# Latent attention: logits from high and low parts, rotated query columns first, values per four heads

## The chip, the cores and the metric

The kernel runs on one core of a Trainium2 chip. The metric is device time in microseconds. The kernel before took 2329.86 us (median of three runs, 2329.52 to 2330.2). Engines are named as the profile names them: PE is TensorE's matrix product, PEld its weight load, DVE is VectorE, ACT is ScalarE, POOL is GpSimd and SP is SyncE, which here only issues DMAs.

## The reference

The reference is a long chain: a first block (sparse attention, a pooling mixer, a mixture of 16384 experts), then two layers with residuals. The second of these layers has the latent attention (`mla`), the only part that the change touches. The sequence has 512 tokens, the model width is 1024, everything is fp32.

```python
proj = u @ w_in                                  # 384 | 256 | 32 | 1024 columns
cq, ckv, k_rope, z = split(proj)
q  = (rms_norm(cq, q_norm) @ w_qb).reshape(B, S, 16, 64 + 32)   # nope | rope
kv = (rms_norm(ckv, kv_norm) @ w_kvb).reshape(B, S, 16, 64 + 64) # k_nope | v
q_rope, k_rope = rotate(q_rope), rotate(k_rope)  # k_rope is shared by the 16 heads
logits = (qn @ k_nope.T + qr @ k_rope.T) * 96 ** -0.5
o = softmax(logits) @ v                          # for each of 16 heads
y = (o * silu(z)) @ w_out
```

So each of 16 heads has a 512x512 logit matrix over 96 columns, no mask, a softmax over keys, and a product with 64 value columns.

## The kernel before, in words

A matrix product of full fp32 operands takes two pieces on PE. The kernel avoids that for its large products: an operand is split into a high part, rounded to the type float32r (FR in the code), and a low part, the difference. ACT writes the high part by a copy, DVE or POOL subtracts to get the low part, and `mm3` (line 152) adds three one-pass products, high by high, high by low and low by high. `panel` (line 142) loads a block of weights, up to 256 rows by 512 columns, and splits it; three raw panels (WB) and four split ones (WS) can be held at once. `linear_tm` and `linear_fm` (lines 180 and 188) run such a projection with tokens or features on the partitions, and call an `evac` function for each finished part.

The logits of the latent attention are the exception: keys and queries are plain fp32 tiles of 96 rows (64 nope rows, 32 rotated), and line 1154 makes one logit block of 128 queries by 512 keys with one fp32 product, which the profile shows as two pieces.

The stage runs as follows. After the z projection (`evac_z`), the normed latents cq and ckv are transposed (`latents`, called between the value parts). The value projection makes all 16 heads' values in two calls of 512 columns, into the tiles vB: 64 high columns and 64 low columns for each head and token block. `four_heads` (line 1133) makes keys and queries of four heads: first the key projection (`evac_k`), then the query projection (`evac_q`), whose three parts of 128 columns are two of nope columns and one, the last, with the rotated columns of the four heads. That last part goes through a rotation: three DVE operations, an addition on POOL (line 1124), and eight DMAs on SP's queue (line 1127) that move the rows into the four query tiles. KB = 6 key tiles and as many query tiles form two rings.

`b_head` (line 1146) runs one head in four units of 128 queries. A unit is: the logit product into a PSUM tile, a maximum on DVE (1156), an exponential on ACT that also sums (1158), four transposes on PE (1161), a high part on ACT (1163) and a low part on DVE (1164). After two units, PE multiplies by the values (1170). Each head ends with a copy, an addition and a reciprocal; every second head also transposes four blocks of zB (1192) and multiplies by them.

The loop over heads calls `four_heads(j + 1)` ahead of the third head of each four (`m == 2`), so that it can be worked on beside the heads. The order on each engine is not written by hand: a planner walks the program with its own estimate of times and gives each engine its next instruction by readiness and by the order in the source. On the chip each engine then follows its own list strictly. PSUM tiles are tagged: `acc` has four buffers, for projections, transposed exponentials and outputs alike; `lg` and `tp` have two each, for logits by turns.

After the heads come the output projection (w_out) with its weights loaded early, a per-layer-embedding step `ple`, and the final norm; they reuse tiles of the stage by tag.

## Time and profile before

| | |
|---|---|
| median of three runs | 2329.86 us |
| the profiled execution, its own time | 2336.29 us |
| its span (first to last instruction) | 2334.1 us |
| granted TensorE clock, mean share of full | 0.984 |
| busy: PE, DVE, ACT, POOL | 2241.3, 1623.3, 1114.2, 1051.2 us |
| latent attention, start of the values to the last value product | 2034 to 2219.8 us |

The durations of single instructions come from the one profiled execution. PE's products are pipelined: a product's own length is longer than the time from one to the next, so costs on PE are read from the distance between starts or from the chain of waits, which counts each piece only as long as it holds the chain. "Granted clock" is the share of 2.4 GHz that TensorE got in a stretch.

### The profile page before, as it was taken

How to read it: one execution, taken by the hardware profiler on the slowest of the kernel's cores; microseconds unless marked ns; L12 is line 12 of the kernel's file. 1: busy time of each engine (PE TensorE's matmuls, PEld its weight loads, DVE VectorE, ACT ScalarE, POOL GpSimd, SP SyncE). 2: the span in 40 equal slices, each digit the busy share in tenths (PEclk: the TensorE clock that was granted, in tenths of full speed). 3: DMA queues.
4: the chain of work that ended last, by engine and by line, in shares of the span. 5: the costliest groups of instructions: out<-in, count | busy, mean ns of one | idle time of the engine just before them, and what ended most of it. 6: DMA issues, size and time to landing. Idle time of an engine off the chain costs nothing.

```text
span 2334.1 us, 32581 instructions
## 1 busy us (share of the span) xinstructions
PE 2241.3 (96%) x11610; PEld 1930.8 (83%) x11610; DVE 1623.3 (70%) x2962; ACT 1114.2 (48%) x2134; POOL 1051.2 (45%) x642
## 2 busy tenths in 40 slices
PE   7999999998999899999999999999999999989998
PEld 5777778988999899999997788887889789767676
DVE  7695447889585654888887988888565445347755
ACT  3656323436757675333332333333456444467742
POOL 4874034574545565778876655564110100121100
PEclk9999999999999999999999999999999999999999
DMA  7465122376767788999998999996410233211121
GB/s 277 145 204 184 60 77 79 124 236 207 257 244 259 247 297 308 341 342 342 334 336 303 340 327 342 327 336 234 129 39 18 82 108 97 74 49 53 33 82 63
DMA packets 206482, 463.04 MB, mean 198 GB/s; under 512 B 17680, under 2 KB 99056, under 8 KB 203248
## 3 DMA queue, kind: packets, MB, share of 16 engines
q1 hardware_dynamic: 169456, 326.72, 41.9%
q0 software_dynamic: 36864, 134.23, 15.8%
q8 instruction: 92, 1.51, 0.3%
q14 instruction: 70, 0.57, 0.1%
HBM read 415.26 MB, written 44.58 MB: 197 GB/s over the span
## 4 chain that ended last, share of the span: by engine, by line
PE 70%; DVE 9%; DMA 6%; issue 6%; POOL 4%; ACT 3%; SPq 0%; POOLq 0%; DVEq 0%; ACTq 0%
PE acc L155 16%; PE acc L154 16%; PE acc L153 15%; PE gp L680 3%; PE tp L155 2%; PE tp L154 2%; PE tp L153 2%; PE lg L154 2%; PE lg L153 2%; PE lg L155 2%; DMA g<-in_peer_v_dram,idx 2%; PE lg L1154 2%; DVE oh L666 1%; POOL wada L271 1%; POOL wlo L716 1%
## 5 line engine op out<-in xcount | busy, mean ns | idle before, releaser
L716 POOL TENSOR_TENSOR wlo<-wraw,whi 128x1024 fp32r<-128x1024 f32 x172 | 441.7, 2570 | 397.0 <-ACT whi L715 388.2
L715 ACT ACTIVATE whi<-wraw 128x1024 fp32r<-128x1024 f32 x256 | 268.9, 1051 | 153.5 <-PE lg L154 73.2
L153 PE MATMUL acc<-fm,whi 128*128 128x384 f32 (+2 forms) x932 | 333.3, 359 | 1.6 <-ACT av L728 1.3
L155 PE MATMUL acc<-fm,wlo 128*128 128x384 f32 (+2 forms) x932 | 322.5, 348 | 3.0 <-POOL wlo L716 2.9
L154 PE MATMUL acc<-fm,whi 128*128 128x384 f32 (+2 forms) x932 | 323.1, 347 | 0.0
L751 DVE CUSTOM_DVE_ANT_0 g<-g,h20y 128x1024 f32<-128x1024 f32 x128 | 197.5, 1548 | 120.5 <-DMA g<-in_peer_u_dram,idx 120.3
L790 ACT ACTIVATE wh<-w 128x384 fp32r<-128x384 f32 x128 | 67.2, 525 | 360.2 <-DVE w L787 345.1
L148 ACT ACTIVATE whi<-wraw 128x1024 fp32r<-128x1024 f32 (+5 forms) x142 | 138.4, 981 | 160.4 <-PE acc L155 89.2
L149 POOL TENSOR_TENSOR wlo<-wraw,whi 128x1024 fp32r<-128x1024 f32 (+4 forms) x48 | 104.4, 2183 | 240.1 <-ACT whi L148 231.5
L154 PE MATMUL acc<-wlo,wh 128*128 128x512 f32 x512 | 203.7, 398 | 5.1 <-POOL wlo L716 5.1
L761 DVE SCALAR_TENSOR_TENSOR h20y<-g,act,h20y 128x1024 f32<-128x1024 f32 x127 | 192.5, 1516 | 17.7 <-DMA g<-in_peer_v_dram,idx 17.2
L155 PE MATMUL acc<-whi,wl 128*128 128x512 f32 x512 | 204.0, 398 | 0.0
L153 PEld LDWEIGHTS acc<-fm,whi 128*128 128x128 f32 x932 | 178.3, 192 | 11.6 <-issue 2.2
L149 DVE TENSOR_TENSOR wlo<-wraw,whi 128x1024 fp32r<-128x1024 f32 (+3 forms) x94 | 109.2, 1169 | 113.1 <-ACT whi L148 109.5
L155 PEld LDWEIGHTS acc<-fm,wlo 128*128 128x128 f32 x932 | 177.7, 191 | 11.4 <-POOL wlo L716 4.2
L154 PEld LDWEIGHTS acc<-fm,whi 128*128 128x128 f32 x932 | 178.4, 192 | 9.0 <-issue 2.2
L734 POOL DMA_INDIRECT g<-in_peer_u_dram,idx x128 | 172.9, 1351 | 26.5 <-issue 14.5
L734 POOL DMA_INDIRECT g<-in_peer_v_dram,idx x128 | 160.7, 1255 | 34.6 <-issue 21.5
L153 PE MATMUL acc<-whi,wh 128*128 128x512 f32 x512 | 171.7, 396 | 0.5 <-ACT whi L715 0.4
L669 ACT ACTIVATE oh<-oh,gT 128x128 f32<-128x128 f32 x384 | 120.1, 392 | 77.4 <-DVE oh L666 77.2
L153 PE MATMUL acc<-whi,fm 128*128 128x512 f32 (+3 forms) x368 | 135.9, 375 | 3.3 <-ACT fm L139 2.1
L791 DVE TENSOR_TENSOR wl<-w,wh 128x384 fp32r<-128x384 f32 x128 | 113.2, 884 | 35.9 <-ACT wh L790 33.9
(367 smaller groups left out, 5512.8 us busy)
## 6 DMA issues: line engine op xcount, KB each, us to landing
wraw<-in_uT_dram SPq DMA_DIRECT2D x128, 512.0 KB
wraw<-in_peer_v_dram SPq DMA_DIRECT2D x128, 512.0 KB
wada<-in_w_adaT_dram SPq DMA_DIRECT2D x48, 512.0 KB
G_d<-stage SPq DMA_DIRECT2D x24, 1024.0 KB
gm<-G_d SPq DMA_DIRECT2D x64, 384.0 KB
A_d<-av SPq DMA_DIRECT2D x88, 192.0 KB
am<-A_d SPq DMA_DIRECT2D x88, 192.0 KB
wraw<-in_w_in_dram SPq DMA_DIRECT2D x24, 512.0 KB
```

The source lines that it names most:

```text
L148: nc.scalar.activation(hi[:, :nk, :n], raw[:, :nk, :n], AF.Copy)
L149: eng.tensor_sub(lo[:, :nk, :n], raw[:, :nk, :n], hi[:, :nk, :n].bitcast(FT))
L153: nc.tensor.matmul(o, lh, rh, start=first, stop=False)
L154: nc.tensor.matmul(o, lh, rl, start=False, stop=False)
L155: nc.tensor.matmul(o, ll, rh, start=False, stop=last)
L669: nc.scalar.activation(oh[:, 1, i], oh[:, 1, i], AF.Copy, scale=gT[:, q * 4 + i:q * 4 + i + 1])
L715: nc.scalar.activation(hi, raw, AF.Copy)
L716: eng.tensor_sub(lo, raw, hi.bitcast(FT))
L734: tc.keep_in_program_order(nc.gpsimd.indirect_dma_start(out=g, out_offset=None, in_=src, in_offset=bass.IndirectOffsetOnAxis(ap=idx0[:, s: ...
L751: nc.vector.tensor_tensor_reduce(out=g, in0=g, in1=h20, scale=1.0, scalar=0.0, op0=OP.mult, op1=OP.add, accum_out=act0[:, i:i + 1])
L761: nc.vector.scalar_tensor_tensor(y, g, act0[:, s:s + 1], y, op0=OP.mult, op1=OP.add)
L791: nc.vector.tensor_sub(wl, w, wh.bitcast(FT))
```

## The change

Keys and queries become tiles of two parts, `[P, 2, S]` in float32r, high and low; `evac_k` and `evac_q` write the low part with a DVE subtraction after ACT's copy. The fixed rotated key rows are split once for each key tile. The logit product becomes `mm3` over 96 rows. In the weights' layout the rotated query columns come first in a group, and `four_heads` makes queries ahead of keys. The rotation's addition moves from POOL to DVE; its eight DMAs now go to a tile rs, from which ACT and DVE write the high and low rows. KB goes from 6 to 5. The values are made per four heads (256 columns at a time), the first four heads' before the loop and the others' beside `four_heads(j + 1)`, which is now called ahead of the last head of each four (`m == 3`). Some tiles of the tail take other tags.

```diff
-KB = 6
+KB = 5
...
+    def evac_v(vB, t, p):
         v = p.rearrange("p (h d) -> p h d", d=64)
-        nc.scalar.activation(vB[j][t][:, :, 0:64], v, AF.Copy)
-        nc.vector.tensor_sub(vB[j][t][:, :, 64:128], v, vB[j][t][:, :, 0:64].bitcast(FT))
+        to = vB[t // 2][:, t % 2]
+        nc.scalar.activation(to[:, :, 0:64], v, AF.Copy)
+        nc.vector.tensor_sub(to[:, :, 64:128], v, to[:, :, 0:64].bitcast(FT))
+
+    def values(j, then=None):
+        vB = [tmp.tile([P, 2, 4, P], FR, name="vB", tag=("h", "gain")[j % 2], bufs=2) for _ in range(2)]
+        linear_tm(A["b_w_v"][0], 2, j * 256, 256, cT, NT, lambda t, p: evac_v(vB, t, p), k_at=3,
+                  by_part=True, then=then)
+        return vB
...
     def evac_k(kB, m, p):
         for a in range(2):
-            nc.scalar.activation(kB[2 * m + a][0:64], p[a * 64:(a + 1) * 64], AF.Copy)
+            hi, lo = kB[2 * m + a][:, 0], kB[2 * m + a][:, 1]
+            own = p[a * 64:(a + 1) * 64]
+            nc.scalar.activation(hi[0:64], own, AF.Copy)
+            nc.vector.tensor_sub(lo[0:64], own, hi[0:64].bitcast(FT))
 
     def evac_q(qB, m, p):
-        if m < 2:
+        if m:
             for a in range(2):
-                nc.scalar.activation(qB[2 * m + a][0:64], p[a * 64:(a + 1) * 64], AF.Copy, scale=B_SCALE)
+                hi, lo = qB[2 * (m - 1) + a][:, 0], qB[2 * (m - 1) + a][:, 1]
+                own = p[a * 64:(a + 1) * 64]
+                nc.scalar.activation(hi[0:64], own, AF.Copy, scale=B_SCALE)
+                nc.vector.scalar_tensor_tensor(lo[0:64], own, B_SCALE, hi[0:64].bitcast(FT),
+                                               op0=OP.mult, op1=OP.subtract)
             return
...
-        nc.gpsimd.tensor_add(r1, r1, r2)
+        nc.vector.tensor_add(r1, r1, r2)
+        rs = lw.tile([P, S], FT, name="rs", tag="r2", bufs=1)
         for i in range(4):
             for a in range(2):
-                dma(qB[i][64 + a * 16:80 + a * 16], r1[a * 64 + i * 16:a * 64 + (i + 1) * 16])
+                dma(rs[i * 32 + a * 16:i * 32 + a * 16 + 16], r1[a * 64 + i * 16:a * 64 + (i + 1) * 16])
+        for i in range(4):
+            hi, lo = qB[i][64:96, 0], qB[i][64:96, 1]
+            nc.scalar.activation(hi, rs[i * 32:(i + 1) * 32], AF.Copy)
+            nc.vector.tensor_sub(lo, rs[i * 32:(i + 1) * 32], hi.bitcast(FT))
+
+    keys = [lz.tile([P, 2, S], FR, name=f"kB{i}", tag=f"kB{i}") for i in range(KB)]
     for k in keys:
-        nc.scalar.activation(k[64:96], krT, AF.Copy)
+        nc.scalar.activation(k[64:96, 0], krT, AF.Copy)
+        nc.vector.tensor_sub(k[64:96, 1], krT, k[64:96, 0].bitcast(FT))
...
     def four_heads(j):
...
+        linear_fm(A["b_w_q"][0], 3, j * 384, 384, cT, NT, lambda m, p: evac_q(qB, m, p),
+                  eng=nc.gpsimd, by_part=True)
         linear_fm(A["b_w_k"][0], 2, j * 256, 256, cT, NT, lambda m, p: evac_k(kB, m, p), k_at=3,
                   eng=nc.gpsimd, by_part=True)
-        linear_fm(A["b_w_q"][0], 3, j * 384, 384, cT, NT, lambda m, p: evac_q(qB, m, p),
-                  eng=nc.gpsimd, by_part=True)
...
-                nc.tensor.matmul(lg, q[:, t * P:(t + 1) * P], k, start=True, stop=True)
+                c = slice(t * P, (t + 1) * P)
+                mm3(lg, q[0:96, 0, c], q[0:96, 1, c], k[0:96, 0], k[0:96, 1], True, True)
...
-    for j in range(2):
-        linear_tm(A["b_w_v"][0], 2, j * 512, 512, cT, NT, lambda t, p, j=j: evac_v(j, t, p), k_at=3,
-                  by_part=True, then=None if j else latents)
-    after = four_heads(0)
+    vB = values(0, latents)
+    after = *four_heads(0), vB
     for j in range(4):
-        kB, qB = after
+        kB, qB, vB = after
         for m in range(4):
-            if m == 2 and j < 3:
-                after = four_heads(j + 1)
+            if m == 3 and j < 3:
+                after = *four_heads(j + 1), values(j + 1)
             h = 4 * j + m
-            b_head(h, kB[m], qB[m])
+            b_head(h, kB[m], qB[m], vB)
...
-    a["b_w_q"] = np.concatenate([wq[..., :64].reshape(384, 4, 256), wq[..., 64:80].reshape(384, 4, 64),
-                                 wq[..., 80:].reshape(384, 4, 64)], axis=-1).reshape(1, 384, 1536)
+    a["b_w_q"] = np.concatenate([wq[..., 64:80].reshape(384, 4, 64), wq[..., 80:].reshape(384, 4, 64),
+                                 wq[..., :64].reshape(384, 4, 256)], axis=-1).reshape(1, 384, 1536)
```

## Rows read from the trace of the kernel before

**Rows 1.** Busy time of the engines on the page.
```profile
PE 2241.3 (96%) x11610; PEld 1930.8 (83%) x11610; DVE 1623.3 (70%) x2962; ACT 1114.2 (48%) x2134; POOL 1051.2 (45%) x642
```
**Rows 2.** Windows: stretch, length; busy PE, PEld, DVE, ACT, POOL; clock, DMA, GB/s.
```profile
2000.00:2050.00 50.00, 48.92 (x217) 38.51 (x215) 14.43 (x21) 22.62 (x39) 5.49 (x4) 1.00 0.19 57
...
2034.00:2062.80 28.80, 22.46 (x103) 17.26 (x102) 10.49 (x18) 16.23 (x30) 9.48 (x7) 0.98 0.26 76
2062.80:2080.50 17.70, 17.70 (x77) 11.09 (x78) 11.24 (x19) 10.72 (x26) 1.23 (x2) 0.85 0.05 11
2080.50:2105.00 24.50, 24.28 (x127) 18.02 (x126) 14.74 (x25) 17.83 (x39) 6.56 (x6) 1.00 0.19 57
2105.00:2120.20 15.20, 14.84 (x87) 10.69 (x86) 12.27 (x22) 11.33 (x27) 1.23 (x2) 1.00 0.01 2
2120.20:2145.70 25.50, 24.24 (x124) 17.75 (x123) 15.63 (x26) 18.11 (x38) 6.33 (x5) 1.00 0.23 73
2145.70:2160.70 15.00, 14.79 (x86) 10.64 (x85) 12.23 (x22) 11.17 (x27) 1.22 (x2) 1.00 0.19 72
2160.70:2188.00 27.30, 24.80 (x127) 18.02 (x126) 19.20 (x28) 18.91 (x39) 3.48 (x3) 1.00 0.21 68
2188.00:2203.00 15.00, 14.77 (x87) 10.63 (x85) 12.25 (x22) 11.16 (x27) 1.23 (x2) 1.00 0.00 1
2203.00:2219.80 16.80, 15.56 (x93) 11.19 (x91) 12.59 (x22) 11.09 (x26) 1.23 (x2) 1.00 0.00 1
```
**Rows 3.** Groups by shape, 2020 to 2235: busy us, mean ns; idle before.
```profile
L1154 PE MATMUL lg<-kB,qB 96*128 96x512 f32 x128 | 66.9, 621 | 8.5 <-DMA qB<-r 7.1 <-ACT L L1158 1.2
...
L1164 DVE TENSOR_TENSOR pl<-tp,ph 128x512 fp32r<-128x512 f32 x32 | 22.0, 687 | 2.8 <-ACT ph L1163 2.4
...
L1163 ACT ACTIVATE ph<-tp 128x512 fp32r<-128x512 f32 x32 | 19.1, 596 | 10.0 <-PE tp L1161 9.6
...
L1110 ACT ACTIVATE kB<-acc 64x512 f32<-64x512 f32 x16 | 9.4, 590 | 0.4 <-PE acc L155 0.3
...
L140 DVE TENSOR_TENSOR fm<-tp,fm 128x256 fp32r<-128x256 f32 x4 | 1.6, 418 | 1.4 <-ACT fm L139 1.4
...
L139 ACT ACTIVATE fm<-tp 128x256 fp32r<-128x256 f32 x4 | 1.4, 380 | 0.0
```
**Rows 4.** The chain of waits: start, us held, engine, tile, line.
```profile
2056.36 0.25 PE acc L155
...
2058.81 1.27 POOL r L1124
...
2060.09 0.59 SPq L1127
...
2060.73 1.93 DMA qB<-r
...
2062.80 6.34 PE lg L1154 x8
...
2070.89 1.72 PE lg L1154 x4
...
2101.53 0.81 PE acc L1170 x7
...
2105.03 0.44 PE tp L1192 x4
...
2121.49 0.23 PE acc L153
...
2122.65 0.23 PE acc L155
```
**Rows 5.** Timeline of DVE: start, us, line, operation, count.
```profile
2147.18 1.29 DVE L1156 TENSOR_REDUCE nm<-lg 128x1 f32<-128x512 f32 x2
...
2176.15 3.44 DVE L149 TENSOR_TENSOR wlo<-wraw,whi 128x1024 fp32r<-128x1024 f32 x2
```
**Rows 6.** Timeline of POOL, the same time.
```profile
2176.25 2.25 POOL L1124 TENSOR_TENSOR r<-r,r 128x512 f32<-128x512 f32 x1 [16.51 <-DVE r L1123]
```

More of the change, by code (lines that the diff above doesn't have):

```diff
@@ L1144, in block_kernel, with b_head @@
              [c[:, 5:7].rearrange("p k (b t) -> p (k b) t", b=2) for c in cT]]
-    def b_head(h, k, q):
+    def b_head(h, k, q, vB):
         sm = small.tile([P, 2, NT], FT, name="sm2", tag="sm2")
@@ L1166, in b_head @@
             for b in range(NT):
-                v = vB[h // 8][b][:, h % 8]
+                v = vB[b // 2][:, b % 2, h % 4]
                 steps = [(o[:, c], v, ph[:, b]), (o[0:64, c], v[:, 0:64], pl[:, b])]
@@ L1199, in block_kernel @@
     nT = lz.tile([P, 8, S], FR, name="nh", tag="zB"), lz.tile([P, 8, S], FR, name="nl", tag="oB")
-    pf = [lz.tile([P, 2, S], FR, name=n, tag=tag) for n, tag in (("pfh", "vB1"), ("pfl", "vB2"))]
-    ple_split(1, lz.tile([P, 2, S], FT, name="pT", tag="vB0"), pf)
+    pf = [lz.tile([P, 2, S], FR, name=n, tag=tag) for n, tag in (("pfh", "kB1"), ("pfl", "kB2"))]
+    ple_split(1, lz.tile([P, 2, S], FT, name="pT", tag="kB0"), pf)
     _, make_n = normed_parts("ple_norm_g_2", 1, nT)
@@ L1217, in final @@
                 dma(out.rearrange("b (t p) d -> p (b t) d", p=P)[:, t, c], h[:, c])
-    ple(1, nT, pf, [lz.tile([P, D], FT, name="pw", tag=tag) for tag in ("vB3", "ph", "pl", "rope")],
+    ple(1, nT, pf, [lz.tile([P, D], FT, name="pw", tag=tag) for tag in ("kB3", "ph", "pl", "rope")],
         lambda t: lw.tile([P, 512], FT, name="sg", tag=("L", "L", "r1", "r2")[t], bufs=(2, 2, 1, 1)[t]), final)
```

6 lines of the change are left out of this document (1 added, 5 removed).

## The prediction

> **What bounds the kernel now.** I began with the page's busy times: TensorE (PE) is busy for 96% of the span [rows 1], so whatever is taken from it counts, if no other engine takes its place. The change touches one stage, the latent attention, so the second view is a table of that stage by pairs of heads [rows 2]. Its cuts are read from the chain of waits: after each odd head four transposes of zB run, eight such rows in all (one stands in [rows 4], at 2105.03), and they end the pairs. The reader is to see three kinds of stretch. The *quiet* pairs (2105.0, 2145.7, 2188.0) take 15.0 to 15.2 us with PE busy for 14.8, VectorE (DVE) for 12.25, ScalarE (ACT) for 11.2: PE is the limit, but the other two stand close behind. The *loud* pairs (2080.5, 2120.2, 2160.7), in which the next four heads' queries and keys are made, take 24.5, 25.5 and 27.3 us; PE is busy for 24.3 to 24.8 of them and DVE for only 14.7 to 19.2. And the start (2034 to 2062.8) has PE at 22.5 of 28.8 us. The chain of waits shows why: PE's last query product is at 2056.36, then come the rotation on DVE, POOL's add, the issue of DMAs and their landing, and the first logits at 2062.80 [rows 4]: some 6.2 us in which PE has nothing. The granted clock of the next stretch is 0.85 of 2.4 GHz on the mean [rows 2], so part of it ran at the 1.2 GHz level after that idle time: eight logit pieces took 6.34 us, where four take 1.72 later [rows 4], 2.9 us lost.
>
> **The change part by part.**
>
> *Logits.* One logit product is now a pair of fp32 pieces. Four pieces follow each other in 1.72 us [rows 4], so one product is 0.86 us of PE (the 621 ns of one piece [rows 3] is its pipelined length, not its pitch). Three one-pass products of 512 columns replace it. The 96-row form is not in the trace; the nearest row is the projections' product of 128 rows and 512 columns, at a pitch of 0.23 us (six in a row, the first at 2121.49 and the last at 2122.65, so 1.16 us for five steps) [rows 4]. Ends: 0.12 us, the pitch of 256-column products (0.81/7 [rows 4]), and 0.43, that of a piece now. I take 0.232, since columns and type are the same: 0.70 us for one product, 0.16 less. 64 products: 10.4 us of PE, 1.3 us a pair. With the ends the 64 products would change by -32 and +27 us; neither end is near a row of the same columns and type, so I give them no more than a few hundredths.
>
> *Values per four heads.* Before the loop, 2 x 24 products of 512 columns (11.2 us of PE) make all values. Now 24 products of 256 columns (24 x 0.117 = 2.8 us) make the first four heads' and three more such sets sit in the loud pairs. Total PE is the same; 8.4 us leave the start and 2.8 us enter each loud pair. The value panel's low part (128x512) goes to DVE there, about 0.65 us, and the evacuations per set are four ACT copies of 0.38 us and four DVE subtractions of 0.42 us [rows 3].
>
> *Rotated columns first.* The chain query product, DVE rotation (3 operations), add, eight DMAs (one issue takes about 0.59 us, landing 1.93 [rows 4]) was last in a group; now the other two query parts (2 x 9 x 0.232 = 4.2 us of PE), the keys (2.8) and, in the loop, the values (2.8) lie behind it as cover. The add moves from POOL, 1.27 us alone [rows 4] and 2.25 beside DVE work [rows 6], to DVE, about 0.65. Added behind the DMAs: a copy to the tile rs, then per head one ACT copy (about 0.6) and one DVE subtraction (about 0.69). SP still issues the eight DMAs in its order, after any weight panel that the planner put ahead; k's and the value panel's loads may stand behind them, but in the loop panels are fetched a group ahead, limited by raw slots, not by SP.
>
> *Low parts.* For each head a DVE subtraction for keys, one for queries, one for the rotated rows: 12 a group. The trace has the 128x512 subtraction from PSUM at 0.687 us [rows 3]; back to back, two DVE operations take 1.29 us [rows 5], so 0.60 to 0.69 each; I take 0.65. The rotated rows' forms of 32 rows are bounded by nothing and 0.69, and go with the nearest row, as length and not rows set it (key copies of 64 rows: 0.59 on ACT [rows 3], 128-row copies: 0.597 [rows 3]). A group's sum on DVE: 12 x 0.65 + 0.65 (add) + 4 x 0.42 + 0.65 = 10.8 us. ACT gains per group 4 x 0.59 (rotated) + 4 x 0.38 + about 0.6 (value panel) = 4.5 us. The keys' fixed rows (five more subtractions, one copy fewer) lie in the z projection before 2034, where DVE is busy for 14.4 of 50 us [rows 2]: nothing. The key and query ring shrinks from 6 to 5, and the next group is made ahead of the last head of four instead of the third. Four new heads need four free slots: with five, three are free after three heads, so this costs nothing by itself, but only one head's work, not two, is left beside the making. The tail's tiles only change names: nothing, 0.5 us either way.
>
> *The sum by stretch.* Start: V 8.4 less, and the rotation covered. PE then has 2.8 (values) + 2.8 (keys) + 6.3 (queries) + 2.2 (twenty transposes at 0.11) = 14.1 us from 2034.6, so to about 2049. The rotation ends later: the queries' first part at 2044.6, three DVE operations and the add 2.6, two issues 1.2, landing 1.9, ACT copy and DVE subtraction 1.3, so logits at about 2052 in place of 2062.8: -10.8. The idle time before them, 3 us, is half of the present one, and I let the clock stay at 2.4 GHz. First pair: 17.7 to 14.4, -3.3 (2.9 of clock, and 1.3 of logits not quite). Quiet pairs: PE needs 14.8 - 1.3 = 13.5, DVE 12.25; I take 13.9, -1.1 three times. Last pair: -0.8, since its drain stays. Loud pairs: PE 24.3 - 1.3 + 2.8 = 25.8; DVE 14.7, 15.6, 19.2 + 10.8 = 25.5, 26.4, 30.0. So DVE becomes the equal of PE, and in the third, where low parts of the output weights are made early (3.44 us for two [rows 5]), more. DVE stands idle for most of the time in which PE makes queries and keys now, so the low parts have room, but two full engines that feed each other do not mesh: 27.3, 27.8 and 30.0, +7.8 in sum. Together -10.8 - 3.3 - 3.3 - 0.8 + 7.8 = -10.4 us.
>
> This is made against the profiled execution: span 2334.1, its own time 2336.3, which is 6.4 above the median 2329.86. The difference carried to the median gives 2319.5.
>
> **Rivals.** (B) *DVE and POOL block each other in the loud pairs.* DVE's two weight subtractions took 3.44 us [rows 5] while POOL's add ran for 2.25 instead of 1.27 [rows 4, 6]; both read two operands from SBUF. By two maxima of half that size (1.29 us) the two subtractions would take 2.58, so DVE lost 0.9 us and POOL 1.0. The change adds six such DVE operations a group (add, four rotated low parts, value panel) beside POOL's query and key panels. Three collisions of 1 us on a full DVE: 3 us more in each loud pair, -10.4 + 9 = -1.4: 2328.5. Against it: the add, which collided, leaves POOL. The Trainium skill (SBUF — State Buffer, "SBUF: two separate sides") calls the port pair of VectorE and GpSimd an exclusive lock for a whole instruction; the two rows agree with it.
>
> (C) *Slower: the making of a group and the heads run one after the other.* DVE takes its orders in one queue. If the low parts (emitted ahead of the last head) stand in it ahead of that head's maxima, exponentials, transposes and value products wait for the whole of them, with one head left to overlap. A loud pair is then a quiet one, 13.9, plus DVE's making, 10.8 + 2.1 of rotation, plus a restart through maximum, exponential, transposes, copy, subtraction and value products, about 4: 31, and 34.5 in the third. That is +19 over the three; if the start then gains only the values less the keys' copy and low part (8.4 - 1.9 = 6.5) and the clock still falls, -6.5 - 3.3 - 0.8 + 19 = +8.4: 2338. It decides where the loud pairs grow by over 6 us each (18.2/3). For it: DVE at 26 of 26 us. Against it: DVE is idle for some 10 us of each loud pair now.
>
> (D) *The rotated columns are not in fact early*: the planner orders by readiness, and all four token blocks of cq must be transposed before them, so keys may run first and the rotation still ends the start, with the clock fallen. Start -6.5, first pair -1.2, the rest as forecast: -4.0: 2326.
>
> **How the numbers follow.** Forecast 55%, with its own range 2311 (loud pairs at PE's 25.8 + 0.5, -16.6 and some 2 on the start) to 2325; B 17%, D 10%, C 18%. No change is within 0.2%, 4.7 us, which is about what can be told apart here: 2325.2 to 2334.5. Faster: nearly all of the forecast, 0.53, and 0.07 of B and D, 0.60. Slower: 0.15 of C and 0.03 of B, 0.18. Same: 0.22. The range 2309 to 2334 leaves out C and a little at the bottom.
>
> **What would show it.** Right: first logits near 2052 on the old scale with the clock at 1.00 from there; logit products of three pieces with a pitch of 0.23; quiet pairs near 13.9 us; loud pairs near 27 to 28 with DVE busy for 25 or more. Wrong: a pitch of 0.3 or more in the logits; a clock below 0.9 after the start; PE waiting for DVE (key or query low parts, or pl) for over 4 us in a loud pair; loud pairs above 31 us, which alone would make the change slower.

## The result and the profile after

The changed kernel took 2355.17 us (median of four runs, 2350.26 to 2361.75), beside 2330.03 for the kernel before; the ratio is 1.0097, 95% interval [1.0076, 1.0118]. It is slower by about 1%, where 2319.5 was predicted with a range to 2334. The profiled execution took 2361.75 us, its span 2359.9 (before: 2334.1). On the page, TensorE's busy time is what it was, 2242.6 for 2241.3 us, and VectorE has 38.7 us more, beside [rows 1]:

```profile
PE 2242.6 (95%) x11722; PEld 1951.2 (83%) x11722; DVE 1662.0 (70%) x3029; ACT 1125.1 (48%) x2159; POOL 1048.7 (44%) x638
```

The windows of the stage after, cut as in [rows 2] (last copy of z to the first logits, then the eight pairs, then 8 us of the output projection; columns as there):

```profile
2033.84:2053.28 19.44, 15.28 (x79) 12.03 (x79) 10.95 (x21) 12.11 (x26) 6.29 (x5) 1.00 0.21 64
2053.28:2071.49 18.21, 15.73 (x86) 13.17 (x87) 16.24 (x28) 14.53 (x32) 1.23 (x2) 0.91 0.19 56
2071.49:2105.10 33.61, 28.46 (x157) 23.46 (x156) 26.31 (x43) 22.33 (x48) 5.75 (x5) 0.95 0.15 42
2105.10:2120.55 15.45, 13.92 (x95) 11.91 (x94) 12.39 (x22) 11.40 (x28) 1.23 (x2) 1.00 0.00 1
2120.55:2154.28 33.73, 29.47 (x157) 24.62 (x156) 26.18 (x43) 22.01 (x47) 5.75 (x5) 0.90 0.20 63
...
2169.72:2208.64 38.92, 30.05 (x158) 25.54 (x157) 30.08 (x47) 24.43 (x49) 1.23 (x2) 0.87 0.19 61
2208.64:2224.30 15.66, 14.13 (x93) 12.13 (x93) 11.87 (x21) 10.70 (x25) 1.23 (x2) 0.99 0.00 1
2224.30:2243.29 18.99, 14.55 (x100) 12.26 (x98) 13.71 (x23) 12.22 (x28) 1.23 (x2) 1.00 0.09 29
2243.29:2251.29 8.00, 6.80 (x19) 5.39 (x19) 6.19 (x10) 4.75 (x9) 0.00 (x0) 0.58 0.37 131
```

The start went from 30.1 us (2032.66 to 2062.8) to 19.4, as forecast. Everything behind it is longer: the loud pairs 33.6, 33.7 and 38.9 us, the quiet ones 15.4 to 15.7 though TensorE is busy for only 13.9 us of them, the last 19.0. The stage as a whole went from 187.1 to 209.5 us, +22.4 of the span's +25.8.

Where a loud pair loses its time is seen in ScalarE's timeline. In the kernel before, these are the two exponentials on either side of the making of a group (start, us, line, operation):

```profile
2082.76 0.69 ACT L1158 ACTIVATE L<-lg,nm 128x512 f32<-128x512 f32 x1 [1.49 <-DVE nm L1156]
...
2094.70 0.68 ACT L1158 ACTIVATE L<-lg,nm 128x512 f32<-128x512 f32 x1
```

And in the kernel after, with some of what lies between them:

```profile
2080.90 0.69 ACT L1177 ACTIVATE L<-lg,nm 128x512 f32<-128x512 f32 x1 [0.89 <-DVE nm L1175]
...
2085.97 0.59 ACT L1125 ACTIVATE qB<-acc 64x512 fp32r<-64x512 f32 x1 [4.29 <-PE acc L155]
...
2089.29 0.63 ACT L1143 ACTIVATE qB<-rs 32x512 fp32r<-32x512 f32 x1
2089.95 0.60 ACT L1125 ACTIVATE qB<-acc 64x512 fp32r<-64x512 f32 x1
...
2101.65 0.68 ACT L1177 ACTIVATE L<-lg,nm 128x512 f32<-128x512 f32 x1
```

Call the distance between these two exponentials the *gap*: no exponential runs in it, so no head gets past it. The three gaps were 11.9, 12.3 and 12.6 us before, and are 20.8, 20.9 and 24.7 after: +29.6 in sum, and the three loud pairs together grew by 29.1 (77.2 to 106.3). So the growth of the gap is the whole of their loss. It was there before, too: ScalarE's list holds all evacuations of a group between two exponentials. But it cost nothing then, as the windows of the first gap show, before and after (columns as above):

```profile
2082.76:2094.70 11.94, 11.94 (x57) 9.25 (x56) 4.06 (x7) 8.38 (x15) 3.08 (x3) 1.00 0.10 34
```

```profile
2080.90:2101.65 20.75, 17.78 (x86) 14.10 (x84) 16.51 (x26) 12.74 (x25) 4.52 (x3) 0.92 0.20 55
```

Before, TensorE was busy throughout. After, it is idle for 3.0 us of this gap (2.3 and 6.7 of the other two), and the clock is lower. At the pitches of the full clock (0.232 us for a product of 512 columns, 0.117 for one of 256, 0.43 for an fp32 piece, 0.11 for a transpose) its products in the gap come to some 11.9 us before and 14.8 after, by estimate. So of the 8.8 us by which this gap grew some 3 are work, the values above all, and some 6 are waiting and lost clock. TensorE's timeline has the longest of its waits in this gap, in brackets with what ended them:

```profile
2092.10 0.39 PE L153 MATMUL acc<-whi,fm 128*128 128x256 f32 x1 [0.43 <-DVE qB L1126]
...
2094.13 0.50 PE L154 MATMUL lg<-kB,qB 96*128 96x512 f32 x1 [0.82 <-DVE kB L1118]
...
2095.94 0.39 PE L153 MATMUL acc<-whi,fm 128*128 128x256 f32 x1 [1.08 <-DVE vB L1104]
```

All three are ended by VectorE, by low parts of queries, keys and values. VectorE's timeline of the same pair:

```profile
2085.18 0.69 DVE L1175 TENSOR_REDUCE nm<-lg 128x1 f32<-128x512 f32 x1
...
2089.95 1.37 DVE L1144 TENSOR_TENSOR qB<-rs,qB 32x512 fp32r<-32x512 f32 x1 [1.85 <-ACT qB L1143]
2091.36 0.69 DVE L1126 SCALAR_TENSOR_TENSOR qB<-acc,qB 64x512 fp32r<-64x512 f32 x1
2092.08 0.68 DVE L1144 TENSOR_TENSOR qB<-rs,qB 32x512 fp32r<-32x512 f32 x1
```

The maximum of the next unit is there at 2085.87, and its exponential comes 15.8 us later, behind the making in ScalarE's list. VectorE first has pauses, the last of 1.85 us until 2089.95, and then works almost without a break; each of its subtractions needs a copy of ScalarE's first, the moved rows' subtractions stand between those that free an accumulation tile, and TensorE's products wait for these tiles. The windows of that stretch (two neighbours, 5 us each) show the exchange: VectorE full, TensorE not, and its granted clock down to a mean of 0.66, so partly at the 1.2 GHz level, after these waits:

```profile
2090.00:2095.00 5.00, 3.62 (x17) 2.20 (x15) 4.84 (x7) 4.85 (x9) 3.45 (x3) 1.00 0.50 145
2095.00:2100.00 5.00, 4.00 (x18) 3.62 (x19) 4.88 (x9) 2.58 (x6) 0.00 (x0) 0.66 0.21 56
```

### The profile page after: what moved, and what is told of

Its sections match the earlier page's. It is cut to its first block, busy times and chain, and to the rows that moved or that the text cites. A ratio compares the mean times of both kernels' runs of the same rounds, so it can differ in the third digit from the quotient of the medians.

```text
span 2359.9 us, 32875 instructions
## 1 busy us (share of the span) xinstructions
PE 2242.6 (95%) x11722; PEld 1951.2 (83%) x11722; DVE 1662.0 (70%) x3029; ACT 1125.1 (48%) x2159; POOL 1048.7 (44%) x638
## 3 DMA queue, kind: packets, MB, share of 16 engines
q0 software_dynamic: 36864, 134.23, 15.5%
## 4 chain that ended last, share of the span: by engine, by line
PE 65%; DVE 12%; issue 7%; DMA 7%; POOL 4%; ACT 4%; SPq 0%; DVEq 0%; POOLq 0%; ACTq 0%
PE acc L153 15%; PE acc L154 14%; PE acc L155 14%; PE gp L680 3%; PE lg L153 2%; PE lg L154 2%; PE lg L155 2%; PE tp L155 2%; PE tp L154 2%; PE tp L153 2%; DMA g<-in_peer_v_dram,idx 2%; POOL wada L271 1%; DMA wada<-in_w_adaT_dram 1%; POOL wlo L716 1%; PE tp L137 1%
## 5 line engine op out<-in xcount | busy, mean ns | idle before, releaser
L751 DVE CUSTOM_DVE_ANT_0 g<-g,h20y 128x1024 f32<-128x1024 f32 x128 | 195.7, 1534 | 121.2 <-DMA g<-in_peer_u_dram,idx 120.9
L761 DVE SCALAR_TENSOR_TENSOR h20y<-g,act,h20y 128x1024 f32<-128x1024 f32 x127 | 188.0, 1480 | 17.4 <-DMA g<-in_peer_v_dram,idx 16.9
L734 POOL DMA_INDIRECT g<-in_peer_u_dram,idx x128 | 175.7, 1373 | 26.4 <-issue 15.8
L155 PEld LDWEIGHTS acc<-fm,wlo 128*128 128x128 f32 x932 | 177.6, 191 | 11.4 <-POOL wlo L716 4.3
L153 PEld LDWEIGHTS acc<-fm,whi 128*128 128x128 f32 x932 | 178.3, 192 | 10.2 <-ACT av L728 1.8
L153 PE MATMUL acc<-whi,fm 128*128 128x512 f32 (+3 forms) x384 | 143.4, 379 | 11.0 <-DVE vB L1104 6.0
L154 PE MATMUL acc<-wlo,fm 128*128 128x512 f32 (+3 forms) x384 | 143.1, 375 | 0.3 <-DVE wlo L149 0.3
```

The costliest lines, as they stand in the source:

```text
L153: nc.tensor.matmul(o, lh, rh, start=first, stop=False)
L154: nc.tensor.matmul(o, lh, rl, start=False, stop=False)
L155: nc.tensor.matmul(o, ll, rh, start=False, stop=last)
L734: tc.keep_in_program_order(nc.gpsimd.indirect_dma_start(out=g, out_offset=None, in_=src, in_offset=bass.IndirectOffsetOnAxis(ap=idx0[:, s: ...
L751: nc.vector.tensor_tensor_reduce(out=g, in0=g, in1=h20, scale=1.0, scalar=0.0, op0=OP.mult, op1=OP.add, accum_out=act0[:, i:i + 1])
L761: nc.vector.scalar_tensor_tensor(y, g, act0[:, s:s + 1], y, op0=OP.mult, op1=OP.add)
```

## The experiments

All are compared by the stage in one profiled execution of each, from the last copy of z to the last value product (187.1 us before, 209.5 after), and by the ratio to the kernel before on the same chip. A pair that no edit touches repeats within about 0.1 us from kernel to kernel; whole executions of one kernel differ by some us, so the stage is the finer measure, and the ratio says whether the total follows.

| run | start | pairs 1 to 8 | stage | ratio |
|---|---|---|---|---|
| before | 30.1 | 17.7, 24.4, 15.2, 25.6, 15.0, 27.2, 15.0, 16.9 | 187.1 | 1 |
| changed | 19.4 | 18.2, 33.6, 15.5, 33.7, 15.4, 38.9, 15.7, 19.0 | 209.5 | 1.0097 [1.0076, 1.0118] |
| e1 | 19.4 | 15.5, 31.0, 15.5, 32.5, 15.5, 32.6, 15.4, 18.3 | 195.6 | 1.0041 [1.0021, 1.0060] |
| e2 | 21.7 | 16.5, 29.9, 15.4, 29.9, 15.4, 32.5, 15.5, 18.8 | 195.7 | 1.0051 [1.0037, 1.0065] |
| e3 | 19.4 | 18.2, 33.5, 15.4, 33.7, 15.4, 39.0, 15.6, 17.0 | 207.3 | 1.0070 [1.0045, 1.0095] |
| e4 | 30.2 | 13.5, 21.6, 14.9, 23.1, 14.9, 24.9, 13.5, 15.5 | 172.1 | 0.9914 [0.9889, 0.9939] |
| e5 | 18.3 | 15.0, 28.6, 15.2, 28.6, 15.0, 29.3, 15.0, 16.9 | 181.9 | 0.9982 [0.9964, 1.0001] |
| e6 | 18.2 | 15.0, 28.1, 15.2, 28.1, 15.0, 28.5, 15.0, 16.9 | 180.2 | 0.9971 [0.9956, 0.9986] |
| e7 | 26.3 | 15.0, 25.5, 15.2, 27.3, 15.0, 26.0, 15.0, 16.9 | 182.2 | 0.9973 [0.9956, 0.9991] |
| e8 | 21.8 | 14.9, 29.7, 16.2, 27.0, 16.2, 31.2, 16.2, 17.0 | 190.1 | 0.9989 [0.9974, 1.0003] |
| e9 | 22.5 | 16.0, 31.5, 15.4, 33.0, 15.4, 35.4, 15.5, 19.3 | 204.1 | 1.0088 [1.0062, 1.0114] |
| e10 | 19.3 | 13.4, 28.5, 15.4, 28.5, 15.5, 31.4, 15.5, 18.4 | 185.8 | 1.0002 [0.9986, 1.0018] |
| e11 | 25.6 | 15.0, 25.5, 15.2, 25.6, 15.0, 26.0, 15.0, 16.9 | 179.9 | 0.9963 [0.9949, 0.9977] |
| e12 | 30.1 | 15.9, 21.2, 14.8, 22.9, 15.1, 24.7, 13.4, 13.5 | 171.7 | 0.9931 [0.9906, 0.9957] |
| e13 | 30.2 | 11.9, 21.2, 10.9, 22.3, 10.9, 25.4, 10.9, 13.5 | 157.0 | 0.9839 [0.9803, 0.9875] |
| e14 | 30.0 | 17.8, 24.4, 16.3, 24.2, 16.3, 25.0, 14.9, 16.3 | 185.2 | 0.9964 [0.9946, 0.9982] |
| e15 | 19.4 | 16.7, 32.6, 13.3, 32.6, 13.3, 35.0, 13.3, 18.3 | 194.3 | 1.0003 [0.9985, 1.0022] |

**e1: no low parts of keys and queries** (from the changed kernel; TensorE makes as many products, all of high parts, so the logits are another quantity).

```diff
-            nc.vector.tensor_sub(lo[0:64], own, hi[0:64].bitcast(FT))
...
-            nc.vector.tensor_sub(lo, rs[i * 32:(i + 1) * 32], hi.bitcast(FT))
...
-                mm3(lg, q[0:96, 0, c], q[0:96, 1, c], k[0:96, 0], k[0:96, 1], True, True)
+                mm3(lg, q[0:96, 0, c], q[0:96, 0, c], k[0:96, 0], k[0:96, 0], True, True)
```

> The changed kernel without its low parts: keys, queries and rotated rows have only the high part, and the three logit products all read high parts, so TensorE has the same work and VectorE 12 subtractions fewer in each group of four heads. Theory 1 (the 12 subtractions are a lump on VectorE that starves TensorE in the loud pairs): loud pairs fall from 33.6, 33.7 and 39 us to about 27 to 29, total 17 to 22 us under the changed kernel, so near 2335. Theory 2 (copies and subtractions that wait for the moved rotated rows stand ahead of the other evacuations in the lists): the copies still wait, 3 us less in each loud pair, near 2345. Theory 3 (the group is made one head too late): no change, near 2353.

All twelve subtractions a group gone, and the stage is 13.9 us shorter, yet the loud pairs stay at 31.0 to 32.6 with VectorE at only 17.4 to 21.4 us of them. The low parts are not the whole of it.

**e2: the rotated rows are split before they are moved**, by one copy and one subtraction of 128 rows, and the DMAs carry both parts.

```diff
+        nc.scalar.activation(r1.bitcast(FR), r2, AF.Copy)
+        nc.vector.tensor_sub(r2.bitcast(FR), r2, r1)
...
-        for i in range(4):
-            hi, lo = qB[i][64:96, 0], qB[i][64:96, 1]
-            nc.scalar.activation(hi, rs[i * 32:(i + 1) * 32], AF.Copy)
-            nc.vector.tensor_sub(lo, rs[i * 32:(i + 1) * 32], hi.bitcast(FT))
+                dma(qB[i][64 + a * 16:80 + a * 16].bitcast(FT), r12[a * 64 + i * 16:a * 64 + (i + 1) * 16])
```

> The changed kernel, but the rotated rows of four heads are split into high and low part once, 128 rows at a time, before the DMAs move both parts straight into the query tiles. ScalarE and VectorE then wait for no DMA, and each has three operations fewer in a group. Theory 2 (waits for the moved rows block the lists): 4 to 6 us less in each loud pair, 15 in all, near 2338. Theory 1 (the lump): three of 12 subtractions go, 2 us each, near 2347. Theory 3: no change.

13.8 us back, as much as all low parts were worth, with all low parts still made. The loud pairs together have 13.9 us less, more than in e1 (10.2); the start is 2.3 us longer. The three gaps fall to 17.1, 17.1 and 19.6 us. The clock is 1.00 in the loud pairs, whose rows are (two of the three):

```profile
2064.17:2094.11 29.94, 26.08 (x158) 22.30 (x157) 23.45 (x40) 20.22 (x45) 5.34 (x5) 1.00 0.22 56
...
2154.86:2187.41 32.55, 26.76 (x157) 22.23 (x156) 27.20 (x43) 21.47 (x44) 1.23 (x2) 1.00 0.29 79
```

So how the rotated rows reach their tiles matters as much as the number of low parts.

**e3: the tail's input in another tile**, one that is not free before the heads end.

```diff
-    ple_split(1, lz.tile([P, 2, S], FT, name="pT", tag="kB0"), pf)
+    ple_split(1, lz.tile([P, 2, S], FT, name="pT", tag="ph"), pf)
```

> The changed kernel with one tile of the tail moved: pT, the input of the step after the attention, takes the place of ph, which is used until the last head ends, and not that of a key tile that is free earlier. If its load and its copy on ScalarE, which the trace shows in front of the last head's copies, cost the end of the attention 2 to 3 us and TensorE's clock another 2: 3 to 5 us less. If the last pair's 18.9 us are only its drain: no change.

The last pair falls from 19.0 to 17.0 us, and the 8 us behind it have a clock of 1.00 in place of 0.58. In the changed kernel the load of pT goes into a key tile that is free early, and its copy stands in ScalarE's list ahead of the last head's own work; the chain of waits there (columns as in [rows 4]):

```profile
2234.41 4.23 DMA pT<-in_pT_dram
2238.66 1.08 ACT pfh L894
...
2243.33 0.59 ACT ol L1191
...
2247.00 0.43 PE acc L154
...
2250.31 0.23 PE acc L154
```

Products of the output projection took 0.43 us each after this wait and 0.23 later. A change of names was worth some 2 us in the stage and 2.5 behind it in the profiled executions (116.6 us from the last value product to the end, 114.1 in e3); the intervals of the two ratios overlap, so the totals can't confirm it.

**e4: one logit product in one pass** (from the kernel before; keys and queries rounded, so the logits have a lower precision).

```diff
-    keys = [lz.tile([96, S], FT, name=f"kB{i}") for i in range(KB)]
+    keys = [lz.tile([96, S], FR, name=f"kB{i}") for i in range(KB)]
...
-        qB = [lw.tile([96, S], FT, name="qB", bufs=KB) for _ in range(4)]
+        qB = [lw.tile([96, S], FR, name="qB", bufs=KB) for _ in range(4)]
```

> The kernel before, with keys and queries rounded to their high part and one one-pass product for the logits (the low parts are left out): TensorE has 0.63 us less in each of 64 logit products, 40 us in all, and the other engines the same work. If the quiet pairs are bound by TensorE, they fall from 15.0 us to VectorE's 12.25, and the whole by 25 us or more, to 2305 or less. If they are bound by the chain through maximum, exponential, transposes and copies in the order in which the lists have them, they stay at 14.5 to 15, and only the loud pairs and the start gain: 5 to 12 us, 2318 to 2325.

64 products of 0.86 us become 0.23, some 40 us less for TensorE, and nothing is added anywhere. The stage falls by 15.0 us. Two quiet pairs stay at 14.9 with TensorE at 12.5 (the third falls to 13.5): for these two TensorE's saving is worth almost nothing. Here is the ceiling of what this change could bring at the logits, and three products have a quarter of that saving.

**e5 and e6: the changed kernel with the logits in fp32 as before** (no low parts, rows moved straight to the query tiles, the tail's tiles in a space of their own), the group made at m == 3 with KB = 5 (e5), and at m == 2 with KB = 6 (e6, the last two lines below).

```diff
-                mm3(lg, q[0:96, 0, c], q[0:96, 1, c], k[0:96, 0], k[0:96, 1], True, True)
+                nc.tensor.matmul(lg, q[0:96, 0, c], k[0:96, 0], start=True, stop=True)
...
-            if m == 3 and j < 3:
+            if m == 2 and j < 3:
```

> The changed kernel with the logits in one fp32 product as before and no high or low parts of keys and queries: rotated columns first, values per four heads, the next group ahead of the fourth head (m == 3, five slots), the rotated rows moved straight into the query tiles. TensorE's logits cost what they did. If low parts and waits for the moved rows are the whole loss (theories 1 and 2), a loud pair is one of before plus the values, 24.4 + 2.8 = 27.2, the start is 8 us or more shorter, and the whole is 2 to 5 us under the kernel before. If the late making costs by itself (theory 3), the loud pairs stay at 30 or more and the whole is 5 to 10 us above it.

> The kernel of the run before this one, with six slots and the next group ahead of the third head (m == 2) as before the change. Theory 3: loud pairs fall from 30 or more to about 27, the whole to 3 to 8 us under the kernel before. Otherwise: within 2 us of the run with m == 3.

Without the high and low parts, and with the group made as early as before, the rest of the change is a gain: e6 is faster than before (e5's interval takes in 1), and its loud pairs of 28.1 to 28.5 us have TensorE at 26.9 of 28.1. Its gaps are 16.0, 16.0 and 16.4 us long, with TensorE busy for 15.6 of each: a long gap is no loss by itself, only the waiting in it. Making a group one head later, with five slots, costs 1.7 us in all (181.9 for 180.2), not the loud pairs' loss. With the low parts in place the earlier making was not run, so what the late one costs there stays open.

**e7: rotated columns and queries first, alone** (from the kernel before; the sum stays on GpSimd, the values stay ahead of the loop).

```diff
-        linear_fm(A["b_w_k"][0], 2, j * 256, 256, cT, NT, lambda m, p: evac_k(kB, m, p), k_at=3,
-                  eng=nc.gpsimd, by_part=True)
         linear_fm(A["b_w_q"][0], 3, j * 384, 384, cT, NT, lambda m, p: evac_q(qB, m, p),
                   eng=nc.gpsimd, by_part=True)
+        linear_fm(A["b_w_k"][0], 2, j * 256, 256, cT, NT, lambda m, p: evac_k(kB, m, p), k_at=3,
+                  eng=nc.gpsimd, by_part=True)
```

> The kernel before with one part of the change alone: the rotated query columns first and the queries ahead of the keys; POOL still adds, logits, values and the place of the making are as before. If the end of the start is the rotation's chain (6.2 us idle and 2.9 lost at the low clock), most of it goes: 5 to 8 us faster, 2322 to 2325. Rival: the planner puts the rotation's operations behind others, or the keys, now last, take its place as the wait: within 2 us of the kernel before.

Start -3.8 us, first pair 15.0 without a fall of the clock, stage -5.0. The values, moved into the loop, then trade 8.1 us of the start for 2.0 us in each loud pair (e6 beside e7): 2.0 us of the stage in all. But e6 also has the rotation's sum on VectorE; e11 below is the fairer neighbour.

**e8: the best version with all three passes**: e2 and e3, with the next values made one head before the next queries and keys.

```diff
+            if m == 2 and j < 3:
+                vN = values(j + 1)
             if m == 3 and j < 3:
-                after = *four_heads(j + 1), values(j + 1)
+                after = *four_heads(j + 1), vN
```

> The changed kernel with the rotated rows split before they are moved, the tail's tile moved, and the next values made ahead of the third head instead of the fourth. Against the split alone (29.9 us a loud pair, last pair 18.8): the last pair falls to 17; if the values crowd the loud pairs, these fall by 1.5 to 3 us each, 6 to 10 us in all; if what is left of their length is the late making of keys and queries, by less than 1 each and 3 in all.

190.1 us, still 10 above e6, which makes its logits by the fp32 product. Its ratio takes in 1; that its total is better beside before than its stage (+3.0) is not explained.

**e9: split before the move, but in four pieces of 32 rows.**

```diff
+            w = slice(i * 32, (i + 1) * 32)
+            nc.scalar.activation(r1[w].bitcast(FR), r2[w], AF.Copy)
+            nc.vector.tensor_sub(r2[w].bitcast(FR), r2[w], r1[w])
```

> As the changed kernel, with the rotated rows split into high and low before they are moved, as in the run that split them first, but in four pieces of 32 rows (four ScalarE copies and four VectorE subtractions, the number of operations of the changed kernel), so that no copy or subtraction waits for a DMA. Theory A (what the loud pairs lost by the rows' detour is the wait of operations in the lists of ScalarE and VectorE for the moved rows): loud pairs near 30 to 31 us, the stage near 196 to 198 us, as where the split was two operations (195.7). Theory B (it is the number of operations: eight of some 0.65 us in place of two, on two engines that are full there): loud pairs near 33.6 us, the stage near 208 us.

204.1 us, between the two: of the 13.8 us of e2 some 8.4 go by the stage to the six additional operations and 5.4 to the wait for the moved rows. Neither theory alone. The totals of e9 and the changed kernel can't be told apart.

**e10: split first, and no low parts** (each product takes high parts alone).

```diff
-                mm3(lg, q[0:96, 0, c], q[0:96, 1, c], k[0:96, 0], k[0:96, 1], True, True)
+                mm3(lg, q[0:96, 0, c], q[0:96, 0, c], k[0:96, 0], k[0:96, 0], True, True)
```

> As the changed kernel, with the rotated rows made single-pass numbers by one copy before they are moved, and no low part made at all: each of the three logit products takes high parts alone, so that its sums are another quantity. TensorE's work is that of the changed kernel. Theory A (with the detour gone, what is left over the version with products in two passes, 181.9 us, is VectorE's subtractions of the low parts): the stage near 180 to 184 us, loud pairs near 27 to 28 us. Theory B (what is left is the shape that the three products and double-width operands give the lists, not the subtractions): within 3 us of the version that splits first and keeps the low parts (195.7 us), loud pairs near 29 to 30 us.

185.8 us: the low parts are worth 9.9 us of the stage once the detour is gone: 2.4 in the start, 3.1 in the first pair, 4.0 in the loud pairs, 0.5 in the last. So the loud pairs have less than half of it. The first pair's part is TensorE's clock. Its row in e2, and then in e10:

```profile
2047.72:2064.17 16.45, 16.45 (x87) 14.26 (x87) 12.24 (x21) 10.98 (x26) 1.23 (x2) 0.80 0.17 42
```

```profile
2047.13:2060.51 13.38, 13.38 (x87) 11.92 (x88) 10.85 (x19) 11.85 (x29) 1.23 (x2) 1.00 0.29 79
```

TensorE is busy throughout both. Ahead of the first logits it had waited 3.94 us for the moved rows in e2, and 1.53 in e10. What is left over e5 is 3.9.

**e11: e7 with the rotation's sum on VectorE.**

```diff
-        nc.gpsimd.tensor_add(r1, r1, r2)
+        nc.vector.tensor_add(r1, r1, r2)
```

> The kernel before with the rotated columns made first and, beside it, the sum of the two rotated products on VectorE in place of GpSimd; keys, queries and values otherwise as before. Theory A (the sum on GpSimd, which runs into the move of the rows, is what a group's first logits still wait for): start some 3 us shorter than with the move alone (26.3 us), the stage near 178 to 180 us, ratio near 0.996. Theory B (the rows arrive early enough in either place): start and stage within 1 us of the move alone (182.1 us), ratio near 0.997.

The stage is as theory A had it, but not where: the start is 0.6 us shorter, the fourth pair 1.7. Beside this version, which has the sum on VectorE as e6 has, the values in the loop bring nothing: the start is 7.4 us shorter in e6, its loud pairs together 7.7 longer, the stage 180.2 for 179.9. This is the fastest version with fp32 logits, and it is faster than the kernel before by 0.37% [0.23, 0.51]; beside e6 and e7 it can't be told apart by the total.

**e12: e4 with each head's output copy, sum and transposes behind the next head's first two units.**

```diff
+            if t0 == 0 and pend:
+                pend.pop()()
...
+        pend.append(finish)
```

> The kernel before with one logit product in one pass (a lower precision of the logits), as the run before with that edit, and with each head's output copy, its sum and the transposes of the finished pair issued behind the first two units of the next head instead of ahead of them. Theory A (a quiet pair's length is set by these operations standing ahead of the next head's maxima in the lists of ScalarE and VectorE): quiet pairs fall from 14.9 to about 13 us, the stage from 172.1 to some 165 us. Theory B (it is the chain from maximum to exponential to transposes within the units, with two buffers): quiet pairs stay at 14.5 to 15 us, the stage within 2 us of 172.1.

As theory B had it: two quiet pairs are at 14.8 and 15.1, and the stage is 0.4 us shorter. The order of the output copy does not set the quiet pairs.

**e13, e14, e15: the maximum left out**, in e4, in the kernel before, and in the changed kernel.

```diff
+    nmc = small.tile([P, 1], FT, name="nmc", tag="nmc", bufs=1)
+    nc.gpsimd.memset(nmc, -1.0)
...
-                nm = small.tile([P, 1], FT, name="nm1", tag="nm1")
-                nc.vector.tensor_reduce(nm, lg, axis=AX.X, op=OP.max, negate=True)
...
-                nc.scalar.activation(L, lg, AF.Exp, bias=nm, accum_out=sm[:, 0, t:t + 1])
+                nc.scalar.activation(L, lg, AF.Exp, bias=nmc, scale=0.125, accum_out=sm[:, 0, t:t + 1])
```

> The kernel before with one logit product in one pass and without the maximum of the logits: the exponential takes a constant bias and a scale of 0.125 that keeps it finite, so it is not the softmax of the reference. A unit loses its VectorE operation of some 0.65 us (5.2 us a pair, of 13.1) and a link of its chain. Theory A (VectorE's maximum, as a link of the chain and as load, paces the quiet pairs at 14.9 us): they fall to about 13 us, where TensorE (12.5) and ScalarE (12.3) are full; loud pairs fall by 1 to 3 us from 21.6, 23.1, 24.9. Theory B (ScalarE and the order of its list pace them): 14.4 to 14.9 us.

> The kernel before without the maximum of the logits (constant bias and a scale of 0.125 in the exponential, so it is not the softmax of the reference). VectorE's work in a quiet pair falls from 12.25 to about 7 us; TensorE keeps 14.8. If TensorE is the bound of the quiet pairs before, as the prediction had it, they stay at 14.8 to 15.0 us and the loud pairs at 24.3 to 27.2. If the chain through the maximum sets them as much as TensorE does, they fall by over 0.5 us.

> The changed kernel without the maximum of the logits (constant bias and a scale of 0.125 in the exponential, so it is not the softmax of the reference). VectorE's work falls by some 5.2 us in each pair. Theory A (what the loud pairs lost is above all VectorE's load, whose list is full while it lasts): loud pairs fall by 5 us or more, from 33.6, 33.7, 38.9 to about 28, 28, 31; quiet pairs fall from 15.5 to about 14. Theory B (it is waits of the lists for the moved rows, and load adds little): loud pairs stay above 31 us.

The quiet pairs answer clearly. A row of e4 (with the maximum):

```profile
2089.74:2104.66 14.92, 12.55 (x84) 10.06 (x83) 13.05 (x23) 12.27 (x29) 1.23 (x2) 1.00 0.00 1
```

one of e13 (the same without it):

```profile
2092.23:2103.10 10.87, 10.58 (x78) 9.03 (x77) 7.68 (x14) 10.77 (x27) 1.23 (x2) 1.00 0.01 2
```

one of e14 (the kernel before without it):

```profile
2096.80:2113.11 16.31, 16.30 (x93) 11.64 (x91) 8.65 (x15) 12.22 (x29) 1.23 (x2) 1.00 0.01 2
```

and a quiet and a loud pair of e15 (the changed kernel without it):

```profile
2067.16:2099.74 32.58, 28.93 (x157) 24.66 (x156) 22.52 (x35) 21.94 (x47) 5.75 (x5) 0.90 0.15 43
2099.74:2113.03 13.29, 13.29 (x95) 12.08 (x94) 7.76 (x14) 11.19 (x27) 1.23 (x2) 1.00 0.00 1
```

Before, TensorE does set the quiet pairs: without the maximum it is busy throughout, and six pairs (second to seventh) take 121.1 us in place of 122.4, only cut at other places (single quiet pairs of 16.3 are no loss). With less TensorE work the maximum takes over, as a link between logits, exponential and transposes or as work for VectorE (12.4 us of the changed kernel's 15.4; the runs don't part the two): e4's 14.9 us fall to 10.9, where TensorE and ScalarE are both full, the changed kernel's 15.4 to 13.3, all of it TensorE's work. The loud pairs behave otherwise: VectorE is busy for 3.8, 3.6 and 5.4 us less, which took only 1.0 and 1.1 us from the first two (theory B), and 3.9 from the third; the gaps stay at 21.7, 21.7 and 24.1 us. Only three of the eight maxima stood in the first pair's gap, so the run hardly thins what VectorE does there. In the first two pairs, then, what counts is the chain of copies and subtractions in the gap, not VectorE's work over the whole pair; in the third that work counts too.

**The ladder.** Put in order, the versions part the whole way from e6 to the changed kernel; each step holds in this order only:

| step | stage | total, ratio to before as us of 2336 |
|---|---|---|
| e6: fp32 logits, rotated first, values in the loop | 180.2 | -6.8 |
| e5: group made one head later, rings of 5 | +1.7 | +2.6 |
| e10: three products, two-part tiles, the tail's tiles back in the key tiles | +3.9 | +4.7 |
| e2: the low parts | +9.9 | +11.4 |
| e9: eight small operations for the rotated rows in place of two | +8.4 | +8.6 |
| changed: these behind the move | +5.4 | +2.1 |

The two columns agree step by step within 3.3 us, and in sum (29.3 and 29.4). Each ratio's interval is 3 to 6 us to either side, so the totals bear out the sum and the large steps, not the small ones. In the three loud pairs alone (77.2 us before) e6 is at 84.8, and the steps add 1.7, 1.9, 4.0, 7.6 and 6.3 us, to 106.3. The step to e10 has 1.4 us in the last pair, where e3 shows what the tail's tiles cost.

## Why the prediction was wrong

Term by term, forecast against measured, in us of the profiled stage: start -10.8, -10.7; first pair -3.3, +0.5; quiet pairs -3.3, +1.4; loud pairs +7.8, +29.1; last pair -0.8, +2.1. Sum -10.4 against +22.4.

**Right.** The start: the first logits came at 2053.28, which is 2052.1 on the old scale (forecast 2052), with the clock at 1.00 until there, though not from there on. The pitch of the logit products: 0.23 us, three to a block, as in the chain of the quiet pair below. TensorE's need in a quiet pair: 13.3 us (e15), forecast 13.5. The values' price in the loop: e6's loud pairs are 2.0 us over e7's and 2.5 over e11's on the mean, forecast 2.8. VectorE's operations: 0.68 to 0.69 us each, also at 32 rows, and its busy time in the loud pairs 26.3, 26.2 and 30.1, forecast 25.5, 26.4 and 30.0.

**The step that failed: "DVE stands idle for most of the time in which PE makes queries and keys now, so the low parts have room".** The sum of VectorE's work was right and the conclusion was not. That idle time is the gap: VectorE has little to do in it (4.1 of 11.9 us before) because no head runs, and it ends when the last tile of the group is evacuated. Work put there lengthens it where a product waits for it. A tile of accumulation was free after ScalarE's two copies; now it needs copy, subtraction, copy, subtraction, on two engines by turns, and among these stand eight operations for the moved rows. I had asked only whether VectorE's total fits beside TensorE's. e15 shows that the total hardly mattered in the first two loud pairs; e9 and e2 show that the number and the place of the operations did.

In the sum it is the loud pairs' +7.8 that was mis-sized: it measured +29.1. e6, without low parts, has +7.6. Of the 21.5 us above that, in the order of the ladder, the low parts as such have 4.0. The rotated rows' small operations and their place behind the move have 13.9, and for these the sum had VectorE's busy time and a small allowance for meshing, but no wait. The other 3.6 came with the late making and the three products from two-part tiles. (A small slip beside it: five slots leave four free after three heads, not three, which changes nothing.)

Of the rivals, C was the mechanism: the making of a group and the heads run one after the other. Its condition, loud pairs that grow by over 6 us each, was met (9.2, 8.1, 11.7). Its price was too low (31, 31 and 34.5 us against 33.6, 33.7 and 38.9), since it added VectorE's work to a quiet pair and left out that ScalarE and VectorE alternate, the wait for the moved rows, and the fall of TensorE's clock after the waiting. Its start was wrong in the other direction. I had given it 18% with "DVE is idle for some 10 us of each loud pair" as what speaks against it, which was the same misreading. The distance between two exponentials in the timeline before, 12 us, would have shown that making and heads already ran one after the other, at no cost then, since TensorE was busy throughout. One part of C was not as it had it: the maximum of the next unit did not stand behind the low parts in VectorE's list; it was there at 2085.87, and it was the exponential that waited, in ScalarE's.

**Quiet pairs.** "PE is the limit" was true at 14.8 us of work. The forecast let TensorE stay the limit down to 13.9, although the note that the other two engines "stand close behind" was there. The chain of the changed kernel's first quiet pair leaves TensorE at 2110.94, and comes back to it at 2112.28:

```profile
2110.49 0.45 PE tp L1180 x4
...
2112.03 0.21 ACT L L1177
2112.24 0.04 issue
2112.28 0.66 PE tp L1180 x4
...
2114.47 0.23 PE lg L153
2114.70 0.23 PE lg L154
2114.93 0.24 PE lg L155
```

TensorE's timeline has two waits in this pair, for an exponential and for a high part; together they are the 1.5 us by which the pair is longer than TensorE is busy:

```profile
2112.28 0.66 PE L1180 MATMUL tp<-ident,L 128*128 128x128 f32 x4 [1.36 <-ACT L L1177]
...
2118.55 0.39 PE L1189 MATMUL acc<-ph,vB 128*128 128x256 f32 x1 [0.17 <-ACT ph L1182]
```

e12 shows for the one-pass version that moving the output copy alone doesn't help; e13 and e15 that taking the maximum out does. Why a quiet pair is 15.4 us here and 14.9 in e4, where VectorE is busy for more of it (13.1 us, here 12.4), stays open.

**First pair.** The clock did not stay up, as the forecast had it: its mean over the pair was 0.91 (0.85 before), and for two microseconds it was at the 1.2 GHz level, after TensorE had waited 2.26 us for the first exponential:

```profile
2058.60 0.87 PE L1180 MATMUL tp<-ident,L 128*128 128x128 f32 x4 [2.26 <-ACT L L1177]
```

```profile
2060.00:2062.00 2.00, 2.00 (x8) 1.60 (x8) 1.91 (x4) 1.13 (x4) 0.00 (x0) 0.50 0.00 0
```

It did not set the length: in e3, which has the same work there, the clock was 0.81 and the pair 18.2 us all the same. VectorE had the first group's low parts to finish among the first maxima: it was busy for 16.2 of 18.2 us. Without them (e1) the pair took 15.5, and with the rows split first as well (e10) 13.4, under the forecast of 14.4.

**Last pair.** "The tail's tiles only change names: nothing": e3 shows 2.0 us for it. A tile's name decides when it is free, hence when the load into it is issued, and where the copy that reads it falls in ScalarE's list.

**Rival B** happened, and is small. GpSimd's row beside VectorE's 1.37 us at 2089.95 above is

```profile
2088.93 3.25 POOL L149 TENSOR_TENSOR wlo<-wraw,whi 128x768 fp32r<-128x768 f32 x2 [8.46 <-PE acc L155]
```

The same subtraction took 0.68 at 2092.08, as GpSimd's came to its end, so one collision cost 0.7 us. The second loud pair has another such (1.42 us at 2138.92), the third none. The Trainium skill (SBUF — State Buffer, "SBUF: two separate sides") has the pair of ports as an exclusive lock; this row agrees with it. By these rows the collisions explain some 1.5 of the 29 us. **Rival D** did not happen.

## What to carry to other kernels

An engine that is idle while another works is not free room if it is idle because its own work can't begin: look for the longest distance between two steps of the inner loop (here two exponentials), see which engine waits in it, and count what is added between them link by link, not as a share of an engine. Split rows before they are moved, in one operation over all partitions, since 32 rows cost what 128 do. And a saving on the busiest engine is worth only as much as its distance to the next limit: leave out one link of the loop's chain (here the maximum) to see where that limit stands before spending work on another engine to relieve the first.

## What the runs showed of the hardware that was not expected

TensorE's busy time in the profile depends on its waits: the same 95 products of a quiet pair count 13.92 us in the changed kernel, where some of them wait, and 13.29 in e15, where none does. A stretch that looks 90% full of TensorE work had more room than that. An operation on 32 rows took about as long as one on 128 rows with as many columns. On VectorE a subtraction of 32x512 took 0.68 us above, where one of 128x512 took 0.687 [rows 3]. On ScalarE 16 copies of 32x512, which read SBUF, took 628 ns each on the mean; 16 of 64x512 from the accumulation tile took 587, and 32 of 128x512 from a tile of transposes 596 (the groups of the changed kernel by shape):

```profile
L1182 ACT ACTIVATE ph<-tp 128x512 fp32r<-128x512 f32 x32 | 19.1, 596 | 13.1 <-PE tp L1180 12.8
...
L1143 ACT ACTIVATE qB<-rs 32x512 fp32r<-32x512 f32 x16 | 10.0, 628 | 0.4
...
L1117 ACT ACTIVATE kB<-acc 64x512 fp32r<-64x512 f32 x16 | 9.2, 587 | 3.4 <-PE acc L155 2.5 <-DVE kB L1118 0.7
```
